# Seven half-size products instead of eight for 28 of the 40 column blocks of an input projection, with two intermediate results parked in DRAM and the spatial mixing moved under the output projection

## The chip, the core and the metric

The kernel runs on one core of one Trainium2 chip. The time is device microseconds (us) of one execution on that core. Before the change three runs took 1326.22, 1326.7 and 1324.02 us, median 1326.22 us. A profiled execution took 1324.03 us; its span from the first to the last instruction is 1322.2 us, with a mean granted TensorE clock of 0.992.

## What is computed

The reference runs two layers over 1,056 tokens (1,024 of a prompt and 32 of a running stream), each token a row of 1,024 float32 numbers. The change is in the first ("even") layer:

```
h = rms_norm(x, g_pre)
z = einsum('btd,de->bte', h, w_in)          # 1024 -> 5120 columns: 40 blocks of 128
a, uv, gate = z[..., :1024], z[..., 1024:3072], z[..., 3072:]
y_a = pool_mixer(a, ...)                    # trailing-window means, per-group linear, scale
u, v = split(gelu(uv));  v = layer_norm(v)
y_b = u * (W_s v + b)                       # spatial mixing over chunks of 128 positions
y = einsum('bte,ed->btd', concat(y_a, y_b) * silu(gate), w_out)     # 2048 -> 1024
x = x + rms_norm(y, g_post)
```

The odd layer (low-rank attention with its own input and output projections) follows and is not changed, apart from the buffers that it starts from.

## The kernel before

Everything lies transposed: channels on the 128 partitions, tokens along the free dimension. The 1,056 tokens are cut into a group "a" of 640 (two PSUM banks of 320) and a group "b" of 416 (one bank). Every product is made to float32 precision from two rounded parts of each operand: `hi` is the value rounded to the matmul's format, `lo` the rest, and hi·hi, hi·lo and lo·hi are summed in PSUM.

`prep_w` (L134) loads a weight block of 128 x 1024 in two pieces of 512 columns through the SP queue, ScalarE casts `hi` (L144), and GpSimd, or VectorE where it is told so, subtracts to get `lo` (L145). `mm_block` (L158) runs one block: 8 pieces of the contraction, 3 part products, 3 matmuls each (320, 320 and 416 columns), thus 72 matmuls, each with its own 128x128 weight load. `evac` (L182) has VectorE multiply the PSUM result by `rep`, the reciprocal root-mean-square of each token, spread over the partitions; `rstd` (L194) makes `rep`.

`even` (L286) goes through the blocks of w1 in this order: 8 and 9 while x arrives (L349-L357), block 10 (L367), the rest of u (11 to 15), v (16 to 23), the gates of half B (32 to 39), the pool inputs (0 to 7) and the gates of half A (24 to 31). v is transposed on TensorE (L424) into one buffer for each of nine token tiles; then `sgu` (L431) takes each tile: layer-norm statistics (L436-L440), normalising (L441), the hi/lo split (L445, L446), the spatial matmuls (L467, L468), a scale and bias by VectorE (L476, L477) and the multiplication of u by GpSimd (L479). This work is interleaved with the blocks of half B's gates and the pool inputs. u, v, the gates and the products stay in SBUF. Then the output projection runs over both halves (K = 16 pieces), first for group "a", then for "b" (L597-L616), and `residual` (L618) adds x, stores x1 to DRAM and makes the next layer's `hi`/`lo`; it runs under the next matmuls.

The order on TensorE is the program's, written by hand (`manual_schedule` on PE); the queues of the other engines are ordered by the framework from its own estimate of when each instruction can start. Side work comes in by tasks: `mm` adds its own price to a clock, `spawn` puts a task on a list with a due time, and `poll`, called after each contraction piece, advances the task that is due:

```
def mm(self, out, lhsT, rhs, start, stop, n):
    self.now += max(n / 2.4, 107)
```

The delays stand in the table `N` in ns of that clock: "lead" is the distance from one token tile of the spatial mixing to the next, "mix" the time from a tile's layer norm to its matmuls, "mixq" the distance between its four groups of matmuls, "tp", "tr", "res", "ra", "rb", "ha", "hb" are those of other tasks.

Of the kernel before, what the change touches and what calls it, by code (L numbers as in the profile page):

```python
# [19 lines left out]
P = 128  # L20
D = 1024
NK = 8
# [12 lines left out]
N = {"x": 462, "mix": 10626, "mixq": 1490, "tr": 717, "lead": 9945, "tr0": 11989, "res": 9194, "ra": 2699,  # L35
     "rb": 1574, "ha": 14000, "hb": 5000, "kv": 429, "q": 20908, "k": 34682, "kvs": 1773, "qs": 10662, "rest": 1357, "r1": 1608,
# [3 lines left out]
LU = 5  # L40
KS = 5
# [30 lines left out]
class Build:  # L72
    def __init__(self, ctx, tc, upto, aps):
        self.ctx, self.tc, self.nc = ctx, tc, tc.nc
        self.upto = upto
        for k, v in aps.items():
            setattr(self, k, v)
        self.uid = 0
        self.now = 0.0
        self.tasks = []  # L80
        self.rr = 0
        self.ca, self.nb = CA, NB
        self.banks = {}

# [35 lines left out]
    def bank(self, tag):  # L120

        tag, bufs = self.banks.get(tag, (tag, 2))
        return self.t(self.ps, [P, 2, 512] if tag in ("za", "sc") else [P, 512], F32, tag, bufs)
# [10 lines left out]
    def prep_w(self, src, n=1024, lo_on=None, pool=None):  # L134
# [3 lines left out]
        for o in range(0, n, 512):  # L138
            m = min(512, n - o)
            raw = self.t(self.stg, [P, 512], F32, "raw", bufs=3)  # L140
# [132 lines left out]
    def new_rep(self):  # L273
        return Pair(self.t(self.cst, [P, NA], F32, "repa"), self.t(self.cst, [P, NB], F32, "repb"))

    def sumsq(self, acc, src, first, g, eng, pool):
        nc = self.nc
        if first:
            nc.scalar.activation(acc, src, AF.Square)
        else:  # L280
            sq = self.t(pool, [P, NA if g == "a" else NB], F32, g)
            nc.scalar.activation(sq, src, AF.Square)
            eng.tensor_tensor(acc, acc, sq, ALU.add)


    def even(self):  # L286
        nc = self.nc
        self.ps = self.open("ps", bufs=2, space=PSUM)
        self.ab1 = self.open("ab1", bufs=24)
        evc = self.evc = self.open("evc")  # L290
        self.ab2 = self.open("ab2", side="right", bufs=9)
        self.V = self.open("V", side="right", bufs=9)


        xs = [self.t(self.V, [P, 1088], F32, "v") for _ in range(NK)]
# [18 lines left out]
        h = [None] * NK  # L314

        def split_x(g, k):
            x = xs[k][:, :NA] if g == "a" else xs[k][:, NA:T]
            if g == "a":
                h[k] = (self.pair(self.ab1, F32R, "a"), self.pair(self.ab1, F32R, "a"))
            else:  # L320
                for i in range(2):
                    h[k][i].b = self.t(self.ab1, [P, NB], F32R, "b")
# [11 lines left out]
        seq = list(range(8, 24)) + list(range(32, 40)) + list(range(8)) + list(range(24, 32))  # L334
        self.pos = 0

        def block(groups="ab", prep=True):
            b = seq[self.pos]
            self.pos += 1
            nb = seq[self.pos] if self.pos < len(seq) else None  # L340
            if prep and nb is not None and nb not in wts:
                wts[nb] = self.prep_w(self.i_w1[nb])
            return self.mm_block(self.wcol(wts[b]), h, range(NK), groups)


        mB = [None] * NK
        mB[0], mB[1] = (self.pair(self.ab2) for _ in range(2))

        for g in "ab":  # L349
            acc = self.t(self.ab2, [P, NA if g == "a" else NB], F32, g)  # L350
            z = [None, None]
            for k in range(NK):
                x = split_x(g, k)
                for i in range(2):
                    z[i] = self.mm_block(self.wcol(wts[8 + i]), h, [k], g, ps=z[i], first=k == 0, last=k == 7)
                self.sumsq(acc, x, k == 0, g, nc.vector, self.ab2)
# [3 lines left out]
        wts[10] = self.prep_w(self.i_w1[10], lo_on=nc.vector)  # L360
        self.pos = 2
        mB[2] = self.pair(self.ab2)
        for g, z in (("a", zz), ("b", z)):
            for i in range(2):
                self.evac(z[i], mB[i], rep, g)
                self.act(mB[i], AF.Gelu, g)
            ps = self.mm_block(self.wcol(wts[10]), h, range(NK), g)  # L367
            self.drain()
            self.evac(ps, mB[2], rep, g)
            self.act(mB[2], AF.Gelu, g)  # L370
        self.pos = 3
        wts[11] = self.prep_w(self.i_w1[11])
        for m in range(3, 8):
            ps = block()
            mB[m] = self.pair(self.ab2)
            self.evac(ps, mB[m], rep)
            self.act(mB[m], AF.Gelu)


        ws = [self.t(self.stg, [P, 512], F32, "raw", bufs=3) for _ in range(2)]  # L380
        nc.sync.dma_start(ws[0], self.i_wsT)
        nc.sync.dma_start(ws[1], self.i_bsb)
        wst = ws[0].rearrange("p (h i) -> p h i", h=4)
        nc.gpsimd.memset(wst[64:128, :, 0:64], 0.0)

        wsp = [self.t(self.ab1, [P, 2, 2, P], F32R, "a") for _ in range(2)]
# [4 lines left out]
        rs = self.t(self.ps, [P, 512], F32, "mi")  # L391
        for e, w in enumerate(wsp):
            for j in range(2):
                nc.tensor.matmul(rs[:, e * 256 : e * 256 + 256], self.ones, w[:, :, j, :], start=j == 0, stop=j == 1)
        Cc = self.pair(self.ab2)

        def cview(m):
            return Cc.a[:, m * P : (m + 1) * P] if m < 5 else Cc.b[:, (m - 5) * P : (m - 4) * P]

        for m in range(NK):  # L400
            hd = slice((m // 2) * P, (m // 2 + 1) * P)
            nc.vector.scalar_tensor_tensor(cview(m), rs[:, hd], self.vec(LNB, m), ws[1][:, hd], ALU.mult, ALU.add)
        rss = self.t(self.ps, [P, 512], F32, "mi")
        for q in range(4):
            for j in range(2):
                nc.tensor.matmul(rss[:, q * 32 : (q + 1) * 32], self.ones[:32, :], wsp[q // 2][:32, q % 2, j, :32],
                                 start=j == 0, stop=j == 1)
        Cs = self.t(evc, [P, NK, 32], F32, "Cs")
        for m in range(NK):
            q = m // 2  # L410
            nc.vector.scalar_tensor_tensor(Cs[:, m, :], rss[:, q * 32 : (q + 1) * 32], self.vec(LNB, m),
                                           ws[1][:, q * P : q * P + 32], ALU.mult, ALU.add)


        vt = {}
        vtok = {}

        def transposes(half, t):
            n = P if t < 8 else 32
            if half == 0:  # L420
                vtok[t] = self.t(self.V, [P, 1088], F32, "v")
            pt = self.t(self.ps, [P, 512], F32, "mi")
            for q in range(4):
                nc.tensor.transpose(pt[:n, q * P : (q + 1) * P], vt[half * 4 + q].tok(t), self.ident)  # L424
            dst = vtok[t][:n, half * 512 : half * 512 + 512]
            if t % 2:
                nc.scalar.copy(dst, pt[:n])
            else:
                nc.vector.tensor_copy(dst, pt[:n])

        def sgu(t):  # L431
            n = P if t < 8 else 32
            v = vtok[t][:n, :D]
# [8 lines left out]
            hi, lo = self.pair(self.ab1, F32R), self.pair(self.ab1, F32R)  # L442
            for g, s in (("a", slice(0, NA)), ("b", slice(NA, D))):
                w = s.stop - s.start
                nc.scalar.copy(hi.get(g)[:n, :w], v[:, s])  # L445
                nc.gpsimd.tensor_tensor(lo.get(g)[:n, :w], v[:, s], hi.get(g)[:n, :w], ALU.subtract)  # L446
            if t == 8:
                for g, s in (("a", slice(0, NA)), ("b", slice(NA, D))):
                    w = s.stop - s.start
                    lg, lb = (self.t(self.ab1, [P, NA if g == "a" else NB], F32, g) for _ in range(2))  # L450
                    nc.sync.dma_start(lg[:32, :w], self.i_lnbc[:, s])
                    nc.sync.dma_start(lb[:32, :w], self.i_lnbc[:, D + s.start : D + s.stop])
                    nc.vector.tensor_tensor(lg[:32, :w], lg[:32, :w], v[:, s], ALU.mult)
                    nc.vector.tensor_tensor(lg[:32, :w], lg[:32, :w], lb[:32, :w], ALU.add)
                    nc.scalar.dma_start(self.o_sv[:, s], lg[:32, :w])
            yield N["mix"]

            for q in range(4):
                mp = self.t(self.ps, [P, 2, 2, P], F32, "mi")
                w = wsp[q // 2][:n, q % 2, :, :n]  # L460
                for i in range(2):
                    m = q * 2 + i

                    def vs(pr):
                        return pr.a[:n, m * P : (m + 1) * P] if m < 5 else pr.b[:n, (m - 5) * P : (m - 4) * P]

                    self.mm(mp[:, i, :, :n], vs(hi), w, True, False, 2 * n)  # L467
                    self.mm(mp[:, i, 0, :n], vs(lo), w[:, 0, :], False, True, n)  # L468
# [4 lines left out]
                for i in range(2):  # L473
                    m = q * 2 + i
                    c = cview(m) if t < 8 else Cs[:, m, :]
# [3 lines left out]
                    nc.gpsimd.tensor_tensor(u, u, tmp[:, i], ALU.mult)  # L479

        def transpose_task(half):
            for t in range(9):
                transposes(half, t)
                yield N["tr"]
            if half:
# [746 lines left out]
```

## Time and profile before

| what | value |
|---|---|
| runs | 1326.22, 1326.7, 1324.02 us |
| the profiled execution | 1324.03 us, span 1322.2 us |
| VectorE, ScalarE and GpSimd busy | 53%, 38% and 29% of the span |
| read from and written to DRAM | 85.49 MB, 18.91 MB |
| w1's blocks after the first three (11 to 39, 0 to 7), with the pool and spatial work among them | 50.51 to 533.7 us |
| output projection | 533.7 to 725.8 us |
| first blocks of the odd layer, group a | 725.8 to 764.6 us |

In the profile PE is TensorE's matmul, PEld its weight load, DVE VectorE, ACT ScalarE, POOL GpSimd, SP the queue that issues loads. A matmul's listed duration holds its passage through the pipeline, and matmuls overlap, so the pace is read from one start to the next. The same holds to a lesser degree for VectorE: the next instruction starts some tens of ns before the end of the one ahead of it.

### The profile page before, as it was taken

How to read it: one execution, taken by the hardware profiler on the slowest of the kernel's cores; microseconds unless marked ns; L12 is line 12 of the kernel's file. 1: busy time of each engine (PE TensorE's matmuls, PEld its weight loads, DVE VectorE, ACT ScalarE, POOL GpSimd, SP SyncE). 2: the span in 40 equal slices, each digit the busy share in tenths (PEclk: the TensorE clock that was granted, in tenths of full speed). 3: DMA queues.
4: the chain of work that ended last, by engine and by line, in shares of the span. 5: the costliest groups of instructions: out<-in, count | busy, mean ns of one | idle time of the engine just before them, and what ended most of it. 6: DMA issues, size and time to landing. Idle time of an engine off the chain costs nothing.

```text
span 1322.2 us, 20987 instructions
## 1 busy us (share of the span) xinstructions
PE 1289.3 (98%) x8152; PEld 1257.9 (95%) x8152; DVE 703.0 (53%) x1370; ACT 496.3 (38%) x974; POOL 389.0 (29%) x443
## 2 busy tenths in 40 slices
PE   9999999999999999999999989999999999999995
PEld 8899999999999999999999989999999999999994
DVE  7311123967956344432286642743666666765438
ACT  7321222322132243322154322434656565655431
POOL 0321212678643222200001354322223323232410
PEclk9999999999999999999999989999999999999998
DMA  5111111111111111222256333322111111116525
GB/s 193 64 49 57 41 41 49 41 40 33 53 40 49 52 41 49 69 75 74 86 185 206 107 116 99 120 82 67 46 44 54 40 54 51 46 50 195 159 88 197
DMA packets 64226, 105.75 MB, mean 80 GB/s; under 512 B 9408, under 2 KB 27232, under 8 KB 64128
## 3 DMA queue, kind: packets, MB, share of 16 engines
q1 hardware_dynamic: 52496, 89.31, 21.9%
q10 hardware_dynamic: 11632, 15.11, 3.2%
q8 instruction: 64, 1.05, 0.3%
q14 instruction: 34, 0.28, 0.1%
HBM read 85.49 MB, written 18.91 MB: 79 GB/s over the span
## 4 chain that ended last, share of the span: by engine, by line
PE 85%; DVE 8%; issue 2%; DMA 1%; POOL 1%; ACT 1%; SPq 0%; ACTq 0%; DVEq 0%; POOLq 0%
PE za L109 36%; PE zb L109 20%; PE sc L109 12%; PE pj L109 11%; PE pj L906 2%; PE mi L109 1%; DMA raw<-in_wout 1%; PE mi L203 1%; PE mi L424 1%; DVE a L1129 1%; ACT sw L830 1%; DVE wlo L145 1%; DVE b L660 0%; DVE b L638 0%; DVE b L649 0%
## 5 line engine op out<-in xcount | busy, mean ns | idle before, releaser
L109 PE MATMUL za<-a,whi 128*128 128x320 f32 x2112 | 463.2, 313 | 2.5 <-DVE a L186 1.4
L109 PEld LDWEIGHTS za<-a,whi 128*128 128x128 f32 x2112 | 371.4, 189 | 5.9 <-DVE a L186 1.8
L144 ACT CAST whi<-raw 128x512 fp32r<-128x512 f32 (+2 forms) x240 | 145.5, 608 | 538.0 <-PE zb L109 255.0
L145 POOL TENSOR_TENSOR wlo<-raw,whi 128x512 fp32r<-128x512 f32 (+2 forms) x166 | 219.1, 1321 | 429.6 <-ACT whi L144 417.2
L109 PE MATMUL zb<-b,whi 128*128 128x416 f32 x1024 | 336.3, 352 | 2.0 <-DVE b L188 1.5
L109 PE MATMUL za<-a,wlo 128*128 128x320 f32 x1056 | 241.5, 310 | 0.0
L109 PEld LDWEIGHTS zb<-b,whi 128*128 128x128 f32 x1024 | 191.4, 188 | 3.3 <-DVE b L188 1.6
L109 PEld LDWEIGHTS za<-a,wlo 128*128 128x128 f32 x1056 | 191.9, 188 | 0.5
L109 PE MATMUL zb<-b,wlo 128*128 128x416 f32 x512 | 179.8, 351 | 1.6 <-DVE wlo L145 1.6
L186 DVE TENSOR_TENSOR a<-za,repa 128x640 f32<-128x640 f32 x38 | 31.1, 820 | 162.7 <-PE za L109 162.7
L879 POOL TENSOR_SCALAR p<-p,nm 128x128 f32<-128x128 f32 (+8 forms) x72 | 53.1, 738 | 163.2 <-DVE nm L878 128.5
L109 PEld LDWEIGHTS zb<-b,wlo 128*128 128x128 f32 x512 | 96.8, 189 | 2.3 <-DVE wlo L145 1.9
L145 DVE TENSOR_TENSOR wlo<-raw,whi 128x512 fp32r<-128x512 f32 x74 | 50.6, 688 | 68.4 <-ACT whi L144 68.2
L211 POOL TENSOR_TENSOR sm<-sm,mhalf 32x1 f32<-32x1 f32 (+3 forms) x17 | 15.6, 926 | 235.7 <-DVE sm L210 235.7
L877 ACT ACTIVATE p<-sc,nm 128x128 f32<-128x128 f32 (+8 forms) x72 | 50.6, 703 | 44.5 <-DVE nm L876 35.1
L109 PE MATMUL sc<-a,whi 128*128 128x400 f32 x256 | 57.6, 346 | 0.2 <-ACT p L877 0.2
L909 DVE TENSOR_TENSOR pl<-pj,ph 128x512 fp32r<-128x512 f32 (+2 forms) x96 | 51.1, 552 | 7.0 <-ACT ph L908 6.3
L876 DVE TENSOR_REDUCE nm<-sc 128x1 f32<-128x128 f32 (+8 forms) x72 | 50.7, 704 | 3.2
L908 ACT CAST ph<-pj 128x512 fp32r<-128x512 f32 (+2 forms) x96 | 43.8, 480 | 20.5 <-PE pj L906 18.1
L109 PEld LDWEIGHTS sc<-a,whi 128*128 128x128 f32 x256 | 46.4, 188 | 0.8 <-ACT p L877 0.4
L109 PE MATMUL pj<-pl,vh 128*128 128x256 f32 (+1 forms) x160 | 45.1, 282 | 0.2 <-DVE pl L909 0.2
L109 PE MATMUL pj<-ph,vl 128*128 128x256 f32 (+1 forms) x160 | 45.0, 281 | 0.0
(285 smaller groups left out, 2251.5 us busy)
## 6 DMA issues: line engine op xcount, KB each, us to landing
raw<-in_w SPq DMA_DIRECT2D x120, 256.0 KB, 2.7
raw<-in_wout SPq DMA_DIRECT2D x60, 256.0 KB, 3.1
gt<-gated SPq DMA_DIRECT2D x32, 128.0 KB, 2.4
ogd<-og ACTq DMA_DIRECT2D x32, 128.0 KB, 2.6
raw<-in_wo SPq DMA_DIRECT2D x16, 256.0 KB, 2.9
raw<-in_wok SPq DMA_DIRECT2D x16, 256.0 KB, 2.7
v<-in_xT SPq DMA_DIRECT2D x16, 208.0 KB, 4.4
rawa<-x1d SPq DMA_DIRECT2D x8, 400.0 KB, 3.7
```

What stands on the lines that cost most here:

```text
L109: self.nc.tensor.matmul(out, lhsT, rhs, start=start, stop=stop)
L144: nc.scalar.copy(hi[:, :m], raw[:, :m])
L145: (lo_on or nc.gpsimd).tensor_tensor(lo[:, :m], raw[:, :m], hi[:, :m], ALU.subtract)
L186: nc.vector.tensor_tensor(two(dst.a), ps[0][:, :, :CA], two(rep.a), ALU.mult)
L203: nc.tensor.matmul(st[:w, j : j + 1], acc[:, j * P : j * P + w], self.one, start=True, stop=True)
L211: nc.gpsimd.tensor_tensor(m[:w, c0:c1], m[:w, c0:c1], self.mhalf[:w, c0:c1], ALU.pow)
L876: nc.vector.tensor_reduce(nm[:n, 0:1], view, axis=AX.XY, op=ALU.max, negate=True)
L877: nc.scalar.activation(pv, view, AF.Exp, bias=nm[:n, 0:1], accum_out=nm[:n, 1:2])
L879: nc.gpsimd.tensor_scalar(p[:n, :K], p[:n, :K], nm[:n, 2:3], 1.0, ALU.mult, ALU.mult)
L906: nc.tensor.transpose(tr[:, e, :], p[:, (b + e) * P : (b + e + 1) * P], self.ident)
L908: nc.scalar.copy(hi[:, :nb, off : off + P], tr[:, :nb, :])
L909: nc.vector.tensor_tensor(lo[:, :nb, off : off + P], tr[:, :nb, :], hi[:, :nb, off : off + P], ALU.subtract)
```

## The change

**Seven products.** 28 blocks of w1 (u 10 to 15, v 16 to 23, the gates 24 to 31 and 34 to 39) are made in 14 pairs. A pair is a 2x2 block product: two output blocks by two halves of the contraction (4 pieces of 128 each), times two halves of the contraction by two halves of the tokens (`HT` = 528). Winograd's form takes seven products of half-size operands. A product (`product`) is 4 pieces x 3 part products x 2 matmuls of `HQ` = 264 columns: 24 matmuls, so 168 for a pair where two blocks had 144. The token-side sums (`th`, `tl`) are made once by `t_prep`; the weight-side sums and their `hi`/`lo` by `s_prep`, three products ahead, all `lo` on VectorE; results go through three PSUM tiles of two banks in turn and are summed by VectorE and ScalarE in `pair_block`, which multiplies by `rep` at the end. Blocks 8, 9, 32 and 33 stay ordinary and run first, blocks 0 to 7 stay ordinary and run last, in the order 6, 7, 4, 5, 2, 3, 0, 1.

**Through DRAM.** The products u·silu(gate) of half B go to `mBd`, the gates of half A to `gAd`, v (transposed as before) to `vd`. They are loaded again where they are used; v has one buffer, so a tile's load waits until the tile before it is split.

**Below the output projection.** The pool blocks now end in the multiplication by the loaded gate and the `hi`/`lo` split (`y_a`). The output projection starts with half A: m = 0 and 1 for group a, with the last pool group's `y_a` between, then m = 2 to 7, m = 2 to 5 (`BOTH`) for both groups. Below these run the loads of u and v and the spatial mixing. When five tiles are done, half B follows for group a and is added to the saved half; the other four tiles, then `split_b`, come below that; last comes group b, with half A's share for m = 6, 7, 0, 1. `residual` and `odd_in` are the same work in other buffers.

The SBUF is laid out in numbered slots (`L`, `R`) instead of rotating pools. The diff, cut to its core:

```
+N = {"tp": 5500, "sa": 9000, "sl": 12000, "sb": 6000, "sbk": 2000, "sg": 500, "x": 462, "mix": 10626, "mixq": 1490, "tr": 717, "lead": 9500, "tr0": 11989, "res": 9194, "ra": 2699,
+     "rb": 1574, "ha": 8000, "hb": 5000, "kv": 429, "q": 20908, "k": 34682, "kvs": 1773, "qs": 10662, "rest": 1357, "r1": 1608,
...
+HT, HQ = 528, 264
+RAW = 3
+LO_POOL = ()
+BOTH = (2, 3, 4, 5)
+A_ORDER = [6, 7, 4, 5, 2, 3, 0, 1]
...
+        def t_prep():
+            for k in range(4):
+                q = [[xs[k + 4 * i][:, j * HT : (j + 1) * HT] for j in range(2)] for i in range(2)]
+                for i in range(2):
+                    nc.scalar.activation(xs[k + 4 * i][:, :T], xs[k + 4 * i][:, :T], AF.Copy, scale=self.vec(GA1, k + 4 * i))
+                tt = nc.vector.tensor_tensor
+                tt(q[0][0], q[0][1], q[0][0], ALU.subtract)
...
+                for n, (j, e, o, f) in place.items():
+                    hi, lo = X[n](k)
+                    src = xs[k + o][:, f * HT : (f + 1) * HT]
+                    nc.scalar.copy(hi, src)
+                    tt(lo, src, hi, ALU.subtract)
+                yield N["tp"]
...
+        pairs = [(10, 11), (34, 35), (36, 37), (12, 13), (14, 15), (38, 39)] + [(24 + 2 * i, 25 + 2 * i) for i in range(4)]
+        pairs += [(16 + 2 * i, 17 + 2 * i) for i in range(4)]
...
+        def s_prep(q):
...
+            if n == 1:
+                for e in ("s1", "s2"):
+                    w[e] = self.t(self.stg, [P, 512], F32, "raw", bufs=RAW)
+                tt(w["s1"], w["21"], w["22"], ALU.add)
+                tt(w["s2"], w["s1"], w["11"], ALU.subtract)
+            elif n == 4:
+                tt(w["21"], w["11"], w["21"], ALU.subtract)
+            elif n == 5:
+                tt(w["s2"], w["12"], w["s2"], ALU.subtract)
...
+            nc.scalar.copy(hi, src)
+            lo_on.tensor_tensor(lo, src, hi, ALU.subtract)
...
+        def product(q, x):
+            out = zt[q % 3]
+            wh, wl = wq.pop(q)
+            s_prep(q + 3)
...
+            for k in range(4):
+                xh, xl = x(k)
+                c = slice(k * P, (k + 1) * P)
+                for j, (w, xx) in enumerate(((wh, xh), (wh, xl), (wl, xh))):
+                    for e in range(2):
+                        self.mm(out[:, e, :HQ], w[:, c], xx[:, e * HQ : (e + 1) * HQ], k == j == 0,
+                                k == 3 and j == 2, HQ)
+                self.poll()
+            return out[:, :, :HQ]
+
+        def pair_block(p, d1, d2):
+
+            a1, b1, a2, b2 = (two(v) for d in (d1, d2) for v in (d[:, :HT], d[:, HT:T]))
+            tt = nc.vector.tensor_tensor
+            q = 7 * p
+            nc.scalar.copy(a1, product(q, X["11"]))
+            tt(b1, product(q + 1, X["t2"]), a1, ALU.add)
+            tt(a1, product(q + 2, X["21"]), a1, ALU.add)
+            nc.scalar.copy(b2, product(q + 3, X["t1"]))
+            tt(a2, product(q + 4, X["t3"]), b1, ALU.add)
+            tt(b1, b1, b2, ALU.add)
+            tt(b2, b2, a2, ALU.add)
+            tt(b1, product(q + 5, X["22"]), b1, ALU.add)
+            tt(d1[:, :T], d1[:, :T], rep.w, ALU.mult)
+            tt(a2, product(q + 6, X["t4"]), a2, ALU.add)
+            tt(d2[:, :T], d2[:, :T], rep.w, ALU.mult)
...
+            if p >= vstart:
+                self.spawn(v_task(p - vstart, d), N["tr0"])
+            elif 24 <= b0 < 32:
+                for e in range(2):
+                    nc.scalar.dma_start(gAd[b0 - 24 + e], d[e][:, :T])
...
+        def load_v(t):
+            n = P if t < 8 else 32
+            vt[t] = R(0)[:, :D]
+            nc.sync.dma_start(vt[t][:n], vd[t, :n])
+
+        load_v(0)
...
+        for k in range(NK):
+            nc.sync.dma_start(mB[k].w, mBd[k])
...
+            nc.vector.tensor_tensor(lo, v, hi, ALU.subtract)
+            if t + 1 < 9:
+                load_v(t + 1)
             yield N["mix"]
...
+        for m in range(2, NK):
+            w = wn.pop(m)
+            if m < 7:
+                wn[m + 1] = self.prep_w(self.i_wout[m + 1, :, :1024])
             else:
...
+            ps = self.mm_block(self.wcol(w), mix, A_ORDER, "ab" if m in BOTH else "a")
+            put(m, ps)
+        while len(done) < 5:
+            self.step(min(self.tasks, key=lambda t: t[:2]))
+        split_a()
```

More of the change, by code (lines that the diff above doesn't have):

```diff
@@ L273, in new_rep, with sumsq @@
     def new_rep(self):
-        return Pair(self.t(self.cst, [P, NA], F32, "repa"), self.t(self.cst, [P, NB], F32, "repb"))
-    def sumsq(self, acc, src, first, g, eng, pool):
+        return self.halves(self.t(self.cst, [P, T], F32, "rep"))
+    def sumsq(self, acc, src, first, g, eng, sq):
         nc = self.nc
@@ L313, in even @@
         rep = self.new_rep()
-        h = [None] * NK
+        h = [tuple(halves(L(2 * k + e, F32R)) for e in range(2)) for k in range(NK)]
         def split_x(g, k):
             x = xs[k][:, :NA] if g == "a" else xs[k][:, NA:T]
[L318 to L322, printed above, removed]
             hi, lo = h[k][0].get(g), h[k][1].get(g)
@@ L332, in even @@
         state = self.t(evc, [P, NK, 30], F32, "state")
[L334 to L343, printed above, removed]
@@ L363, in even @@
+        for i in range(4):
+            s_load(0, i)
         for g, z in (("a", zz), ("b", z)):
             for i in range(2):
[L365 to L377, printed above, removed]
@@ L380, in even @@
[L380 to L383, printed above, removed]
+                self.evac(z[i], u01[i], rep, g)
+                nc.scalar.activation(u01[i].get(g), u01[i].get(g), AF.Gelu)
+            if g == "a":
+                tp = self.spawn(t_prep(), N["tp"])
+            for i in range(2):
+                ps = (zt[i], None) if g == "a" else (None, zt[2][:, i, :])
+                if g == "b" and i == 1:
+                    s_prep(0)
+                    s_prep(1)
+                self.mm_block(self.wcol(wts[32 + i]), h, range(NK), g, ps=ps)
+                if i == 0 and g == "a":
+                    while any(t[2] is not tp[2] for t in self.tasks):
+                        self.step(next(t for t in self.tasks if t[2] is not tp[2]))
+                self.evac(ps, g01[i], rep, g)
@@ new lines, in even, with pslot @@
+        self.h2 = [(Pair(None, None), Pair(None, None)) for _ in range(NK)]
+        zs = [zt[(7 * len(pairs) + i) % 3] for i in range(3)]
+        self.zrot = [[zs[0], zs[2]], [zs[1][:, i, :] for i in range(2)]]
+        self.shut(self.lb)
+        lb = self.lb = self.open("lx")
+        mix = {}
+        pfree, held = list(range(9)), {}
+        def pslot(who, dt=F32):
+            i = pfree.pop(0)
+            held.setdefault(who, []).append(i)
+            return R(i, dt)
+        gslot = dict(zip(A_ORDER, (16, 17, 4, 5, 6, 7, 8, None)))
@@ new lines, in even, with put @@
+        nc.scalar.dma_start(self.o_st, state)
+        yp = self.yp = [halves(L(m)) for m in range(NK)]
+        def put(m, ps):
+            nc.scalar.copy(two(yp[m].a), ps[0][:, :, :CA])
+            if m in BOTH:
+                nc.scalar.copy(yp[m].b, ps[1][:, :NB])
+        part = {}
+        for m in range(2):
+            if m == 1:
+                wA1 = self.prep_w(self.i_wout[1, :, :1024])
+            part[m] = self.mm_block(self.wcol(wA if m == 0 else wA1), mix, A_ORDER[:6], "a", last=False)
@@ new lines, in even @@
+        B2 = zs[1]
+        y_a(pg, wp[pg], lambda: (B2, self.t(self.ps, [P, 512], F32, "mi")))
+        for m in range(2):
+            self.mm_block(self.wcol(wA if m == 0 else wA1), mix, A_ORDER[6:], "a", ps=part[m], first=False)
+            put(m, part[m])
+        wn = {2: self.prep_w(self.i_wout[2, :, :1024])}
+        mB = [halves(L(8 + k)) for k in range(NK)]
+        vt = {}
+        def load_v(t):
+            n = P if t < 8 else 32
+            vt[t] = R(0)[:, :D]
+            nc.sync.dma_start(vt[t][:n], vd[t, :n])
@@ L400, in even @@
[L400 to L407, printed above, removed]
-        Cs = self.t(evc, [P, NK, 32], F32, "Cs")
@@ L409, in even @@
[L409 to L422, printed above, removed]
-            for q in range(4):
[L424 to L429, printed above, removed]
+        Cc = R(8)
@@ L479, in sgu, with sgu_task @@
                     nc.gpsimd.tensor_tensor(u, u, tmp[:, i], ALU.mult)
-        def transpose_task(half):
+            done.append(t)
+        done = []
+        def sgu_task():
+            yield from spatial()
             for t in range(9):
-                transposes(half, t)
-                yield N["tr"]
-            if half:
-                for t in range(9):
-                    yield from sgu_lead(t)
-        def sgu_lead(t):
-            self.spawn(sgu(t), 0)
-            yield N["lead"]
@@ L618, in residual, with split_a @@
-    def residual(self, g, acc, y, h2):
+                self.spawn(sgu(t), 0)
+                yield N["lead"]
+            self.spawn(split_b(), N["sb"])
+        k0 = [halves(R(6 + i, F32R)) for i in range(2)]
+        def split_a():
+            for k in range(NK):
+                hi, lo = (v.a for v in (mix[A_ORDER[k - 1]] if k else k0))
+                mix[8 + k] = (Pair(hi, None), Pair(lo, None))
+                nc.scalar.copy(hi, mB[k].a)
+                nc.vector.tensor_tensor(lo, mB[k].a, hi, ALU.subtract)
```

499 lines of the change are left out of this document (322 added, 177 removed).

## The prediction

> **What bounds the kernel.** I read the page's span, busy shares and chain first, then what TensorE waited for, then a table of stages.
>
> ```profile
> span 1322.2 us, 20987 instructions
> PE 1289.3 (98%) x8152; PEld 1257.9 (95%) x8152; DVE 703.0 (53%) x1370; ACT 496.3 (38%) x974; POOL 389.0 (29%) x443
> PE 85%; DVE 8%; issue 2%; DMA 1%; POOL 1%; ACT 1%; SPq 0%; ACTq 0%; DVEq 0%; POOLq 0%
> ```
> ```profile
> PE mi L203 <- DVE b L660: 5.8, 1, 5.8
> ```
> ```profile
> 34.00:50.50 16.50, 13.53 (x86) 13.15 (x86) 7.74 (x18) 5.86 (x9) 6.27 (x9) 1.00 0.20 65
> 62.16:73.81 11.65, 11.65 (x75) 11.61 (x74) 1.32 (x2) 2.42 (x5) 2.59 (x2) 1.00 0.14 46
> 168.70:313.20 144.50, 144.50 (x942) 143.02 (x941) 86.53 (x166) 38.46 (x66) 69.16 (x82) 1.00 0.13 41
> 646.40:700.00 53.60, 51.55 (x276) 50.08 (x276) 41.67 (x69) 23.92 (x38) 1.57 (x3) 1.00 0.55 175
> ```
>
> TensorE is the bound: busy 98% of the span, 85% of the chain, and its longest wait for another engine is 5.8 us. In the stage table the columns are the stretch, its length, then PE, PEld, DVE, ACT and POOL busy, the granted clock, the DMA share and GB/s. The stretch 62.16 to 73.81 is one clean block of w1: 11.65 us, PE full, DVE idle for nine tenths. So in this stage only fewer or shorter matmuls save time, and DVE has room to pay for it. In the output projection (646.40) DVE is busy 41.67 of 53.60 us and DMA runs at 175 GB/s: there is less room there.
>
> **The products.** Does a matmul of 264 columns cost 264/320 of one of 320?
>
> ```profile
> 154.31 0.46 PE L109 MATMUL za<-a,whi 128*128 128x320 f32 x2
> 154.61 0.34 PE L109 MATMUL zb<-b,whi 128*128 128x416 f32 x1
> 154.79 0.46 PE L109 MATMUL za<-a,whi 128*128 128x320 f32 x2
> ```
> ```profile
> 1192.19 0.28 PE L109 MATMUL pj<-ph,vh 128*128 128x256 f32 x1
> ...
> 1192.91 0.28 PE L109 MATMUL pj<-ph,vh 128*128 128x256 f32 x1
> ```
> ```profile
> 1189.51 0.29 PE L109 MATMUL pj<-qh,wlo 128*128 128x288 f32 x1
> 1189.64 0.29 PE L109 MATMUL pj<-qh,whi 128*128 128x288 f32 x1
> ```
>
> Two of 320 take 0.30 us, one of 416 takes 0.18. Between the first and the last row of 256 columns lie six starts, so 0.72 / 6 = 0.120 us each; 288 columns take 0.13. In between, 264 columns take 0.120 + 8/32 x 0.010 = 0.1225 us. A pair was 2 x 11.65 = 23.30 us; it becomes 168 x 0.1225 = 20.58, a gain of 2.72, and 14 pairs gain 38.1 us. The bounds are the neighbouring rows: at 0.120 a pair is 20.16 (43.9 us gained), at 0.130 it is 21.84 (20.4 us). I take the middle value, since 256 is much the nearer width.
>
> The Trainium skill, "TensorE: Matmul & The Clock Gate", section "Back-to-back issue gap", gives N/2.4 + 2.5 ns; by it a pair would go from 21.5 to 18.9 us, an estimate of 36 us for all. The trace's own pace is some 8% slower than that page's, at every width.
>
> All other TensorE work is the same in number: as many transposes, pool products, spatial matmuls and output columns as before. The stretch 168.70 to 313.20 held 11 blocks (128.2 us by the clean one), so 16.3 us of transposes and spatial work; they move to the v pairs and below the output projection and cost the same there. Taken as 0, with -6 to +6 for waits between them.
>
> **Does VectorE keep up with the pairs?**
>
> ```profile
> 33.48 1.28 DVE L145 TENSOR_TENSOR wlo<-raw,whi 128x512 fp32r<-128x512 f32 x2
> 34.68 1.54 DVE L186 TENSOR_TENSOR a<-za,repa 128x640 f32<-128x640 f32 x2
> ```
> ```profile
> L145 DVE TENSOR_TENSOR wlo<-raw,whi 128x512 fp32r<-128x512 f32 x74 | 50.6, 688 | 68.4 <-ACT whi L144 68.2
> L186 DVE TENSOR_TENSOR a<-za,repa 128x640 f32<-128x640 f32 x38 | 31.1, 820 | 162.7 <-PE za L109 162.7
> L144 ACT CAST whi<-raw 128x512 fp32r<-128x512 f32 x220 | 136.1, 620 | 521.2 <-PE zb L109 243.9 <-PE za L109 97.6 <-issue 87.6
> L192 ACT ACTIVATE a<-a 128x640 f32<-128x640 f32 x32 | 23.6, 739 | 22.6 <-DVE a L186 22.6
> ```
> ```profile
> 34.04 1.28 ACT L192 ACT_TABLE_LOAD   x1
> ```
>
> Two in a row take 1.28 us where one lasts 0.688, so the pace is 0.59 us at 512 columns; in the same way 0.72 at 640, a slope of 1.02 ns per column. That makes 0.61 at 528, 1.15 at 1,056 and 0.49 at 416. A pair asks DVE for 4 sums and 7 `lo` of 512 (6.5 us), 5 sums with PSUM and 2 in SBUF of 528 (4.3) and 2 multiplications by `rep` (2.3): 13.1 us of 20.58. Three pairs add two gate products (2.3), the four v pairs 3 copies (1.8). The last three products of a pair carry most: 3 `lo`, 2 weight sums, 5 token sums, 2 multiplications, 8.3 us (10.6 with gates) against 3 x 2.94 = 8.8 us of PE. PSUM holds three products, so a result may be late by two, 5.9 us, and the next window is light. ACT has 7 casts of 0.62, two copies and two activations of about 1.1, some 8 us, plus a table load of 1.28 us whenever gelu follows silu. All covered on average; the handoffs at a pair's end I price at 0.2 us, 3 us for 14 pairs. Bounds: 0 if all hides, 14 at a microsecond each.
>
> **The entry.** Product 1 needs the token sums of all four pieces. `t_prep` gives DVE 32 instructions of 528 (19.5 us). Until it ends DVE also has the work that the row 34.00 to 50.50 shows (7.7), `lo` of blocks 32 and 33 (4 x 0.59 = 2.4), three more evacuations (1.7), the first three `s_prep` (5 x 0.59 = 3.0) and two gate products (2.3): 36.6 us from 34.0, to 70.6. PE needs two blocks from 35.5 (23.3 us, and 1.7 of `rstd` matmuls) to 60.5, product 0 to 63.4, and the last piece of product 1 at 65.6. A wait of 5 us, 6 with handoffs; 0 if DVE's order is kinder, 15 if ACT's casts hold it up.
>
> After a wait that long the clock may drop:
>
> ```profile
> 764.60:779.50 14.90, 9.10 (x48) 8.80 (x47) 8.54 (x18) 3.85 (x7) 6.13 (x9) 0.77 0.51 155
> ```
>
> Behind the 5.8 us wait the granted clock averages 0.77 over this stretch, but most of the slow time was the wait itself. The Trainium skill, same page, section "Part 1: The HAM clock gate", says that an idle window of about 3.4 us halves the clock until a busy one has passed; by that this entry would cost up to 2 us more. The row agrees, and the upper end takes it in.
>
> **The spatial mixing.** One buffer for v makes each tile a chain: load, statistics, GpSimd's power, normalise, cast, subtract, and only then the next load.
>
> ```profile
> cos<-in_cos SPq DMA_DIRECT2D x1, 528.0 KB, 4.2
> gb<-in_gp2bc SPq DMA_DIRECT2D x1, 512.0 KB, 5.0
> sin<-in_sin SPq DMA_DIRECT2D x1, 528.0 KB, 3.4
> ```
> ```profile
> L436 DVE BATCH_NORM_STATS2 bs<-v 128x6 f32<-128x512 f32 x16 | 10.6, 669 | 1.1 <-ACT v L427 1.1
> L441 DVE TENSOR_SCALAR v<-v,sm 128x1024 f32<-128x1024 f32 x8 | 7.4, 930 | 0.4
> L440 POOL TENSOR_TENSOR sm<-sm,mhalf 128x1 f32<-128x1 f32 x8 | 4.3, 543 | 13.7 <-DVE sm L439 13.7
> ```
>
> Load 4.2 us, two statistics 1.3, aggregate and add 0.3, power 0.5, normalise 0.9, cast of 1,024 1.1 (by the two ACT rows' slope), subtract 1.1: 9.4, with handoffs about 10.3 us. The plan sets tiles 9,500 ns apart on its own clock; a clean block is 24 x 1,056 / 2.4 = 10.56 us on it and 11.65 on the chip, so a tile has 10.5 us. Chain and plan are about equal. The eight loads of u (4.3 MB, 25 us at 175 GB/s) go out around the same time, and tile 1 and the weights of m = 3 queue behind them on SP. I price this at 7 us, nearer to the low end since chain and plan come out equal: 0 if the u loads start early under the last pool product, 27 if each tile takes 14 us (9 x 14 less 99 us of cover: 9 x 10.5 and about 4.5 of lead). Waiting in SP's queue behind a v load are weight loads (PE then waits for them); behind TensorE's wait on a tile stand the output matmuls.
>
> **Joins.** Between half A's first matmuls and the last pool group, and at `split_a`, the `hi`/`lo` of the next piece follow late results: 2 us, from 0 to 6. The group b part brings fewer matmuls over the same `residual` work; its 5.8 us wait stays. Taken as 0.
>
> **The sum**, against the profiled execution's own 1324.0 us: -38.1 + 3 + 6 + 7 + 2 = -20.1, so 1303.9. The runs' median is 2.2 us above that execution, so the forecast for a median is 1306.
>
> **The rivals.**
>
> *All covers hold.* The waits come to 6 us instead of 18: 1324.0 - 38.1 + 6 + 2.2 = 1294. For it speaks that PE was kept 98% busy with DVE at 86.53 of 144.50 us in the mixing stage; against it the entry, where DVE's work adds up to more than PE's.
>
> *The tile chain sets the pace of the output projection* (slower). If a tile takes 16 us (a 5.0 us load, queued behind weights; DVE busy with other tiles' scale and bias), PE waits 9 x 16 - 99 = 45 us: 1324.0 - 38.1 + 11 + 45 + 2.2 = 1344. It decides from 9c - 99 = 27, c = 14 us. For it: load and chain are serial, and the row 646.40 shows DMA and DVE already loaded. Against: the rows add up to 10.3.
>
> *VectorE sets the pace of the pairs* (slower). If a pair takes 23 us, the gain there is 4 and the rest costs 15: 1324.0 - 4 + 15 + 2.2 = 1337. From 22.2 us on nothing is left. For it: the last three products' 8.3 to 10.6 us. Against: two products of slack in PSUM.
>
> *Weight loads set the pace*, so that the change does not do what it says: 168 loads where 144 stood, 27.2 us per pair, 54 us slower, 1399. The 256-column rows, each with a load of its own, start 0.120 us apart and speak against it. The Trainium skill, same page, section "LDWEIGHTS", puts a load of 128 columns at 107 ns, still under that pace.
>
> **The numbers.** A difference of 0.2% (2.7 us) is about what a measurement can tell. Forecast (1299 to 1320) 0.45; all covers hold (1284 to 1299) 0.3; gain eaten up (1320 to 1330) 0.1, of which 0.06 lies within 0.2%; tile chain 0.08, VectorE 0.05, weight loads 0.02. Faster 0.45 + 0.3 + 0.03 = 0.78, same 0.06, slower 0.16. The range leaves out the dearest ends of the slower cases and the cheapest of the fast one: 1288 to 1330.
>
> **What would show it.** Right: 14 stretches of 20 to 21 us for 168 matmuls of 264 columns, starts 0.12 us apart; one wait of some 5 us at product 1 for `lo` of the token sums; small waits below the output projection on v's `hi`/`lo`. Wrong: starts at 0.13 or more; gaps at each pair's end for a PSUM tile that VectorE holds; TensorE waiting at every tile of the mixing; a chain that runs through v's loads.

## The result and the profile after

The changed kernel takes 1367.3 us (median of 4 runs, 1365.11 to 1368.61) where the kernel before takes 1326.46 beside it: a ratio of 1.031, 95% interval 1.029 to 1.0329. It is slower by 40.8 us; the prediction had said 1306 us. The profiled execution took 1365.11 us.

The head of the page after, with span, busy shares and the chain:

```profile
span 1363.2 us, 22025 instructions
...
PE 1269.6 (93%) x8488; PEld 1228.1 (90%) x8488; DVE 860.6 (63%) x1613; ACT 552.2 (41%) x1027; POOL 306.0 (22%) x381
...
PE 25%; DVE 3%; issue 1%; ACT 1%; DMA 1%; POOL 0%; DVEq 0%; ACTq 0%; POOLq 0%
```

TensorE fell from 98% to 93% busy, and its share of the chain from 85% to 25%. The percentages of the chain after no longer add up to the span: the chain is followed back from one release to the next and here it breaks off, so it says little, and the waits have to be read instead. What TensorE waited for, after (total, times, longest):

```profile
PE z L116 <- DVE l L199: 15.3, 9, 5.6
PE z L116 <- DVE r L589: 7.1, 7, 1.2
PE z L116 <- DVE l L856: 5.9, 4, 3.1
PE mi L214 <- DVE r L907: 5.3, 1, 5.3
PE z L116 <- DVE l L854: 5.3, 3, 3.7
PE z L116 <- DVE b L623: 4.9, 4, 1.6
```

Before, the only long wait was one of 5.8 us. Now TensorE waits for VectorE in ordinary blocks: L199 and L589 are evacuations, in the odd layer's gates and in the pool blocks. The stage table after (stretch, length, PE, PEld, DVE, ACT and POOL busy, clock, DMA share, GB/s) shows where that happens and where it doesn't:

```profile
35.87:46.45 10.58, 10.55 (x62) 10.32 (x62) 9.16 (x22) 8.20 (x12) 7.30 (x6) 0.84 0.01 3
64.70:289.60 224.90, 224.90 (x1849) 224.90 (x1849) 163.58 (x234) 86.78 (x127) 0.00 (x0) 1.00 0.26 91
356.90:486.60 129.70, 115.60 (x705) 111.43 (x704) 75.92 (x105) 30.14 (x57) 38.63 (x45) 1.00 0.25 79
663.10:741.90 78.80, 64.09 (x315) 60.46 (x315) 49.27 (x84) 29.98 (x48) 8.22 (x10) 0.93 0.50 159
826.40:948.00 121.60, 106.58 (x638) 103.42 (x636) 48.10 (x99) 34.07 (x61) 28.85 (x36) 0.96 0.24 78
```

The second row holds the first eleven pairs: PE is full for 224.90 of 224.90 us, 20.44 us per pair. The third is the pool blocks, which the change was not meant to touch: eight blocks and three `y_a` products. A clean block is 11.65 us and a `y_a` product (half a block) 5.8, so 110.6 us would do (8 x 11.65 + 3 x 5.8); it took 129.7, and VectorE was busy for only 75.92 of them. The fourth row is group b's part of the output projection, and the first belongs to the entry; both are taken up below. The last row is the odd layer's gates, with VectorE busy 40% and TensorE with 15 us of idle time. The timeline of one pool block's start shows what is wrong (start, length, engine, line, operation; in brackets the idle time before it and who ended it):

```profile
368.64 0.46 PE L116 MATMUL z<-l,whi 128*128 128x320 f32 x2
368.65 0.82 DVE L587 TENSOR_TENSOR r<-z,rep 128x640 f32<-128x640 f32 x1 [9.43 <-PE z L116]
369.39 0.55 DVE L588 TENSOR_TENSOR r<-z,rep 128x384 f32<-128x384 f32 x1
369.86 0.18 DVE L589 TENSOR_TENSOR r<-z,rep 128x32 f32<-128x32 f32 x1
370.10 0.94 PE L116 MATMUL z<-l,whi 128*128 128x416 f32 x4 [0.99 <-DVE r L589]
```

Block 7's first two matmuls, for group a, start at 368.64. The third is its first matmul for group b, and it waits until VectorE has read out block 6's group b (384 and 32 columns). Block 7 writes another accumulator than the one that is read: group b has two, in turn. But the changed kernel makes these two out of one PSUM tile. The lines are in the diff, outside the core shown above:

```
+        zs = [zt[(7 * len(pairs) + i) % 3] for i in range(3)]
+        self.zrot = [[zs[0], zs[2]], [zs[1][:, i, :] for i in range(2)]]
```

Of the three two-bank tiles that the products went through, two become group a's accumulators, and the two halves of the third become group b's. Before, `zb` was two tiles of one bank. My theory (A): a matmul into one half is made to wait for the reader of the other half, because they are one tile to the framework that sets the waits, and each block then loses what VectorE needs to read out its predecessor. The rivals (B): the loss is the spatial mixing below the output projection, or VectorE's added work, whoever shares a tile.

### The profile page after: what moved, and what is told of

The parts are those of the page before. It is cut to its first block, busy times and chain, and to the rows that moved or that the text cites. A ratio compares the mean times of both kernels' runs of the same rounds, so it can differ in the third digit from the quotient of the medians.

```text
span 1363.2 us, 22025 instructions
## 1 busy us (share of the span) xinstructions
PE 1269.6 (93%) x8488; PEld 1228.1 (90%) x8488; DVE 860.6 (63%) x1613; ACT 552.2 (41%) x1027; POOL 306.0 (22%) x381
## 5 line engine op out<-in xcount | busy, mean ns | idle before, releaser
L116 PE MATMUL z<-l,whi 128*128 128x264 f32 (+2 forms) x2032 | 395.2, 308 | 31.8 <-DVE l L199 15.3
L116 PEld LDWEIGHTS z<-l,whi 128*128 128x128 f32 x2032 | 319.1, 191 | 39.5 <-DVE l L199 16.6
L116 PE MATMUL z<-l,wlo 128*128 128x264 f32 (+2 forms) x1240 | 269.0, 301 | 0.0
L155 ACT CAST whi<-raw 128x512 fp32r<-128x512 f32 (+1 forms) x180 | 108.1, 603 | 352.5 <-PE z L116 221.1
L116 PEld LDWEIGHTS z<-l,wlo 128*128 128x128 f32 x1240 | 203.5, 191 | 0.3
L116 PE MATMUL z<-r,whi 128*128 128x264 f32 (+2 forms) x696 | 152.8, 307 | 15.6 <-DVE l L854 5.3
L116 PE MATMUL z<-a,whi 128*128 128x320 f32 x704 | 145.2, 312 | 1.5 <-ACT a L625 0.7
L116 PEld LDWEIGHTS z<-r,whi 128*128 128x128 f32 x696 | 114.5, 191 | 19.2 <-issue 4.8
L116 PEld LDWEIGHTS z<-a,whi 128*128 128x128 f32 x704 | 116.1, 188 | 2.9 <-ACT a L625 0.9
L116 PE MATMUL z<-a,wlo 128*128 128x320 f32 x352 | 80.2, 309 | 0.0
```

What stands on the lines that cost most here:

```text
L116: self.nc.tensor.matmul(out, lhsT, rhs, start=start, stop=stop)
L155: nc.scalar.copy(hi[:, :m], raw[:, :m])
```

## The experiments

**Own tiles for group b.** After the products, the pool of PSUM tiles is closed and another opened in its place, with four tiles:

```
-        zs = [zt[(7 * len(pairs) + i) % 3] for i in range(3)]
-        self.zrot = [[zs[0], zs[2]], [zs[1][:, i, :] for i in range(2)]]
+        self.shut(self.zp)
+        self.zp = self.open("zq", space=PSUM)
+        yb = [self.t(self.zp, [P, 512], F32, f"y{i}", 1) for i in range(2)]
+        ya = [self.t(self.zp, [P, 2, 512], F32, f"y{i + 2}", 1) for i in range(2)]
+        self.zrot = [[ya[1], ya[0]], yb]
```

An instruction that had used both halves at once (the last `y_a`'s evacuation, the squares of half B) becomes two. What was expected:

> The seven products are as in the changed kernel; after them, group b's two accumulators are two PSUM tiles of their own instead of the two halves of one tile. Theory A (shared tile: the next block's first group-b matmul waits until the block before it is evacuated, although it writes the other half): the waits of 1.2 us per pool block go, those of the gates and of the output projection's group b mostly too, together some 45 us by the wait table: about 1322 us. Theory B (VectorE is late in these stages, whatever the buffers): the waits stay or move to the next buffer, under 12 us gained: 1355 us or more.

Measured: 1313.02 us (1311.62 to 1314.14), ratio to before 0.9901, interval 0.9884 to 0.9918; 54.3 us less than the changed kernel, and more than the 45 that theory A took from the listed waits (a wait as listed is less than what it costs, see below). The same block start in this run, then its stage table (pool blocks, group b's part of the output projection, gates), then what TensorE waited for:

```profile
371.60 1.13 PE L125 MATMUL y<-l,whi 128*128 128x320 f32 x6
371.61 0.82 DVE L600 TENSOR_TENSOR r<-y,rep 128x640 f32<-128x640 f32 x1 [9.43 <-PE y L125]
...
372.36 0.55 DVE L601 TENSOR_TENSOR r<-y,rep 128x384 f32<-128x384 f32 x1
...
372.58 0.64 PE L125 MATMUL y<-l,wlo 128*128 128x320 f32 x3
```
```profile
359.87:472.00 112.13, 112.13 (x705) 111.36 (x704) 77.52 (x104) 30.36 (x57) 39.53 (x45) 1.00 0.28 92
644.78:711.66 66.88, 59.13 (x314) 56.40 (x314) 51.34 (x85) 29.27 (x48) 8.61 (x10) 0.97 0.58 189
795.16:900.00 104.84, 104.84 (x669) 104.08 (x668) 49.65 (x101) 37.34 (x68) 31.10 (x37) 1.00 0.28 96
```
```profile
PE y L125 <- DVE b L877: 5.6, 1, 5.6
PE mi L223 <- DVE r L924: 5.3, 1, 5.3
PE mi L125 <- DVE tm L780: 4.3, 2, 2.9
PE mi L125 <- DVE dgh L780: 2.5, 2, 1.3
PE mi L125 <- DVE dgl L780: 2.2, 2, 1.6
PE z L125 <- DVE r L206: 2.1, 1, 2.1
PE z L125 <- DVE r L208: 2.0, 1, 2.0
```

Block 7's matmuls run on from 371.60 without a gap (a third of them, with 416 columns, for group b), while VectorE reads block 6: its group a from 371.61, its group b from 372.36 (L601). The pool blocks take 112.13 us with PE full: 17.6 of the 54 us come back here. The gates are full as well, and group b's part of the output projection (the row 644.78) is 12 us shorter. Of the waits at the evacuation of a block, the two at the entry (L206, L208) are left, and some 2 us in group b's output (L871, L873, not shown). The new tiles take the place of the pool that was closed, the matmuls are the same, VectorE is busy for 866.1 us where it was for 860.6, and the mean granted clock is 0.985 where it was 0.984: what goes is the wait. How the framework comes to set it was not looked into; the runs show that sharing a tile decides.

**The other side: one shared tile in the kernel before.** The first trial gave group b's two accumulators of the kernel before as halves of one tile. In it group b of pool blocks 2, 4 and 6 and of the first gate of half A was overwritten by a `y_a` product ahead of its evacuation, by the order of the code, which makes the output wrong; the work is otherwise whole.

```
+        if tag == "zb" and not self.banks:
+            self.zh.append(self.zh.pop(0))
+            return self.zh[-1]
...
+        zh = self.t(self.ps, [P, 2, 512], F32, "zb", 1)
+        self.zh = [zh[:, i, :] for i in range(2)]
```

The edit also replaces tiles that are taken anew for each block by halves that live throughout. The accumulators of the changed kernel live throughout in both of its forms, shared and own, so that alone does not make them wait.

> The kernel before, with one thing changed: group b's two accumulators are the two halves of one PSUM tile. Theory A (shared tile): each block that uses them waits for the evacuation of the block before it. Some 37 blocks of w1, 8 pool products, 8 outputs and 8 gates of the odd layer, 1.2 us each where VectorE is free at once and up to 5 us where it is not: 60 to 110 us slower, 1385 to 1435 us. Theory B (VectorE late whatever the buffers, or something in the new layout): 1326 us, no change.

Measured: 1411.15 us, ratio 1.0634 (1.0595 to 1.0674). A second trial has the same edit behind a change of order (a pool block's evacuation told ahead of the `y_a` product), so that nothing is overwritten, and that order alone is its control.

> The kernel before, with only the order of statements changed, so that in a block that GpSimd evacuates the evacuation is told ahead of y_a's product. The control for the run beside it. Both theories: no difference, 1326 us within 8.

> The control with one edit: group b's two accumulators become the two halves of one PSUM tile in place of two tiles; the computation is whole. Theory A (the shared tile makes each block's first product into one half wait for the evacuation of the other half): slower by 55 to 90 us than the control, 1381 to 1416 us, with waits of about 1 us of TensorE on VectorE at the first group-b product of each block. Theory B (the loss of the changed kernel came from elsewhere, such as the spatial mixing below the output projection or the token sums): 1326 us within 8.

Measured: the control 1326.61 us (ratio 1.0002, 0.9987 to 1.0017), with the shared tile 1411.58 us (ratio 1.0645, 1.0614 to 1.0677). One declaration costs 85 us in a kernel that has none of the rest of the change. TensorE's longest wait in the control, and the main ones with the shared tile:

```profile
PE mi L203 <- DVE b L664: 5.8, 1, 5.8
```
```profile
PE zb L109 <- DVE b L191: 36.2, 31, 5.6
PE zb L109 <- DVE v L525: 8.8, 8, 2.6
PE zb L109 <- DVE v L191: 6.5, 7, 0.9
PE zb L109 <- ACT b L556: 6.4, 7, 1.2
```

In the second fence 53 waits of about 1.1 us stand at `zb`, group b's accumulator: one at nearly every block. They are 57.9 us together. Two more rows of that list stand at `zb`, 4.7 us in six waits (L623) and one of 4.4 (L285), while the control has 3.3 us there in all: 63.7 us more than the control. The wait as listed is less than what a block loses: after, pool block 3 with a wait of 0.99 us took 12.86 us from its first start to the next block's (452.48 to 465.34), and 11.62 with own tiles (443.18 to 454.80), 1.24 more. By that factor 63.7 us of waits are 80 us of time, an estimate, of the 85 measured.

**Without the products.** The kernel with own tiles, but the 14 pairs as 28 ordinary blocks and no token sums.

```
-        def t_prep():
...
+            for e, d in enumerate((d1, d2)):
+                nb = flat[2 * p + e + 1]
+                wts[nb] = self.prep_w(self.i_w1[nb], lo_on=nc.vector)
+                ps = self.mm_block(self.wcol(wts.pop(flat[2 * p + e])), h, range(NK))
+                self.evac(ps, halves(d), rep)
```

> As e1_own_banks, but the 14 pairs are computed as 28 ordinary blocks and the token sums are left out: the new order, the storage in DRAM and the mixing below the output projection without the products. The seven products alone are worth 14 x (23.3 - 20.44) = 40 us less what the entry costs (about 4): 36 us slower than e1. Theory A: about 1358 us. Theory B: about 1395 us.

Measured: 1354.39 us, ratio 1.0215 (1.0194 to 1.0235). The products bring 1354.4 - 1313.0 = 41.4 us. Some 1.7 of it lies at the entry, which ends at 69.4 us here and at 67.7 with the products: in this kernel blocks 32 and 33 have tiles of their own too, and TensorE waits 6.2 us for the spread of `rep` (L241) instead. Everything else that the change does (parking in DRAM, the mixing's new place, the new order) costs 28.6 us over the 1325.75 of the kernel before, even with own tiles.

**Without the spatial mixing.** The kernel with own tiles; v's statistics, its products and the multiplication of u are left out, so u goes on unmixed.

```
-            load_v(0)
...
-                    self.mm(mp[:, i, :, :n], hi[:, c], w, True, False, 2 * n)
-                    self.mm(mp[:, i, 0, :n], lo[:, c], w[:, 0, :], False, True, n)
```

> As e1_own_banks, without the spatial mixing (no loads of v, no layer norm of v, no spatial matmuls, and u times gate goes on unmixed). TensorE loses 14 us of matmuls. If the mixing costs only these, 14 us faster than e1. If VectorE's lateness in the mixing holds TensorE up (theory B: waits of 5 to 12 us in either half of the output projection), 30 us or more faster than e1.

Measured: 1287.04 us, so the mixing costs 26 us where it is, between the two cases that were expected. In the kernel with own tiles a group of four mixing matmuls delays the next block's matmuls by this much:

```profile
540.15 0.35 PE L125 MATMUL y<-b,wlo 128*128 128x416 f32 x1
540.34 0.57 PE L125 MATMUL mi<-r,r 128*128 128x256 f32 x4
540.75 0.50 PE L125 MATMUL y<-a,whi 128*128 128x320 f32 x2
541.09 0.35 PE L125 MATMUL y<-b,whi 128*128 128x416 f32 x1
```

0.41 us to the next start, and 0.04 more to the one after it (0.34 us between the last two rows, where two matmuls of 320 take 0.30): 0.45 us for each of 32 groups, 14.4 us. The four groups of the short ninth tile and the twelve matmuls that set the mixing up take some 4.5 us more, read in the same way. In the list of waits above, 9.0 us stand at `mi` with L780 as their end: the mixing's PSUM bank, which VectorE has still to read. That makes some 28 where 26 were measured; the kernel without the mixing has small waits that the other has not, such as 1.4 us for `whi` (L164). So most of the 26 are matmuls, and about a third is waiting.

**The entry and the scratch.** In the kernel with own tiles, two more places shared a PSUM tile: blocks 32 and 33 for group b were two halves of one product tile, and the squares of the last residual used, as scratch, the tile that the odd layer's first block needs.

```
-                ps = (zt[i], None) if g == "a" else (None, zt[2][:, i, :])
+                ps = (zt[i], None) if g == "a" else (None, zt[2 * i][:, 0, :])
...
-        za = self.zrot[0][0]
+        za = self.zrot[0][1]
```

> e1_own_banks with the two waits of the same kind that are left: blocks 32 and 33 of group b go to two PSUM tiles instead of two halves of one (waits of 2 us at the entry), and the squares of group b's outputs go to the accumulator that the odd layer takes second instead of first (a wait of 5.6 us). Theory A: 7 to 8 us faster than e1, about 1305 us. Theory B: VectorE is late there and the wait moves to the next buffer: under 2 us.

Measured: 1310.43 us (1309.83 to 1311.72), ratio 0.9877 (0.9852 to 0.9901): 2.6 us instead of 7 to 8, and little more than the runs can tell, since the interval overlaps that of the kernel with own tiles. What this kernel waited for in the first pair (64 to 90 us):

```profile
PE z L125 <- DVE r L404: 1.3, 1, 1.3
PE z L125 <- ACT l L403: 0.4, 1, 0.4
```

The 2.0 us at L208 and the 5.6 us at L877 are gone. In their place comes this wait for the token sums at product 1, which takes the first pair from 20.51 to 22.74 us, and in the odd layer's first blocks one of 2.1 us for the spread of its `rstd`. Most of what was freed seems to have been given back at the next thing that was late.

**Less on VectorE.** The last kernel with the `lo` of half B's and group b's output weights on GpSimd.

```
-                wn = self.prep_w(self.i_wout[m + 1, :, 1024:], lo_on=nc.vector)
+                wn = self.prep_w(self.i_wout[m + 1, :, 1024:])
...
```

> e4_entry_scratch with the lo parts of half B's and group b's output weights subtracted by GpSimd instead of VectorE. If VectorE's load sets the pace of the output projection (theory B for this stage: its busy share is 60.7 of 73.7 us in half B's group a), VectorE loses 11 to 12 us there and the stage gets 5 us or more faster. If it is the handing over between engines, no gain, or a loss since GpSimd takes 1.3 to 1.4 us for what VectorE does in 0.6: 0 to 8 us slower.

Measured: 1315.03 us (1311.48 to 1316.03), 4.6 above the kernel that it was made from; the ratios to before, 0.9903 (0.9870 to 0.9935) and 0.9877, overlap in their intervals, so what is shown is that nothing was gained. Its waits from 490 to 705 us:

```profile
PE mi L125 <- DVE dgh L780: 4.6, 2, 3.5
PE mi L125 <- DVE tm L780: 4.1, 2, 3.3
PE y L125 <- POOL wlo L165: 2.3, 2, 1.5
...
PE mi L125 <- DVE dgl L780: 1.4, 2, 0.8
```

VectorE is busy for 145.57 us from 492 to 705 where it was for 158.65, and the waits on the mixing's bank stay at about 10 us; those for GpSimd's `wlo` are new. That speaks against VectorE's work in sum setting the pace of that part. It does not settle it, since GpSimd's lateness came in its place.

**The mixing later.** The plan's clock counts 10.56 us for a block that takes 11.65 on the chip, so it might bring TensorE to the mixing products too early. The delays times 1.103:

```
-N = {... "mix": 10626, "mixq": 1490, ... "lead": 9500, ...
+N = {... "mix": 11720, "mixq": 1640, ... "lead": 10480, ...
```

> The kernel with own tiles for group b and the squares' scratch moved, with the mixing plan's delays raised by 10.3% (11720 for 10625, 1640 for 1490, 10480 for 9500). Theory A (the plan's clock runs some 10% ahead of the chip, 10.56 us against 11.65 us a block, so TensorE comes to the mixing products before VectorE has freed the mixing's PSUM bank): the waits on the mixing's bank, 4.3 and 2.5 us in the output projection, go, and the kernel gains 3 to 5 us on 1310.4, to 1306. Theory B (VectorE has too much to do in that stage, wherever the products are put): 1310 within 2, the waits move to other products.

Measured: 1310.46 us (1309.51 to 1312.56), no difference. From 480 to 660 us the waits on the mixing's bank:

```profile
PE mi L125 <- DVE dgl L780: 5.3, 3, 2.2
PE mi L125 <- DVE dgh L780: 2.4, 2, 1.4
PE mi L125 <- DVE tm L780: 0.8, 1, 0.8
```

Without the edit the three were 4.3, 2.4 and 2.2 us, for `tm`, `dgh` and `dgl`: 8.9 us became 8.5, on other products. The plan's clock is not the cause. Neither of these two runs found what is; that VectorE comes to these short reads late because longer work (statistics, normalising, residual) stands ahead of them in its queue fits the rows but was not tried.

## Why the prediction was wrong

**The step that failed** is "All other TensorE work is the same in number [...] Taken as 0, with -6 to +6 for waits between them", and with it "The group b part [...] Taken as 0". The number was right (8,488 matmuls in the profile after and with own tiles alike, the 8,152 of before and 14 x 24 for the products); the waits were not. The change also altered which PSUM tile the untouched blocks accumulate in, a part that the prediction did not list and so did not price. It costs 54.3 us, shown from both sides: taken out of the changed kernel, and put into the kernel before, where it costs 85. None of the rivals held it. The likeliest of the slower ones, at 1344 us, was a chain through v's loads; none of TensorE's listed waits after is for a load. The nearest that the prediction came was its sign "gaps at each pair's end for a PSUM tile that VectorE holds": such gaps came, but in the blocks that were not to change.

The Trainium skill, "PSUM — Partial Sum Buffer", section "PSUM bank collisions raise a hardware error", asks for a guard between engines by bank and quadrant, and says that accesses to different banks run clean. The two halves here were different banks, and the run with own tiles in the same place agrees: VectorE reads group b's one bank from 372.36 us while TensorE goes on into the other without a gap. So the wait was not one that the memory asked for.

**The products: right.** From 119.76 to 120.86 us the profile after has nine starts of 264 columns:

```profile
119.76 0.28 PE L116 MATMUL z<-l,whi 128*128 128x264 f32 x1
119.88 0.40 PE L116 MATMUL z<-r,whi 128*128 128x264 f32 x2
120.12 0.41 PE L116 MATMUL z<-l,wlo 128*128 128x264 f32 x2
120.37 0.65 PE L116 MATMUL z<-l,whi 128*128 128x264 f32 x4
120.86 0.41 PE L116 MATMUL z<-l,wlo 128*128 128x264 f32 x2
```

1.10 / 9 = 0.122 us, where 0.1225 was said. A pair takes 20.44 us (20.58 said), so 14 pairs gain 14 x (23.30 - 20.44) = 40.0 us (38.1 said), and the run without products gives 41.4. The rivals of weight loads and of VectorE's pace fall: the profile after lists no wait of TensorE between 64 and 357 us, and VectorE is 73% busy over the first eleven pairs. The 3 us of handoffs were 0.

**The entry: size near, cause another.** 6 us were said for a wait at product 1. With own tiles the first pair starts at 67.72 us, after four blocks; before, three blocks ended at 50.51, and a fourth would end at 62.16. That is 5.6 us, but they came from the shared tile of blocks 32 and 33 (the 2.0 us at L208) and from a slower clock (below). The forecast wait showed as 1.7 us only when that sharing was taken away, so the size was near by luck.

**The mixing: 9 us of waits where 7 were said, of another kind.** So the size is luck. They are at the mixing's PSUM bank, and no wait is for a load or for v's `hi` and `lo`.

**Joins and group b.** 2 us were said for joins and 0 for group b. At the first join 1.2 us of waits are listed with own tiles (L637, L640, L641). Group b's twelve half blocks would take 54.7 us at 4.56 each (24 matmuls of 416 columns at 0.19 us); with own tiles they take 66.88, 12 us more, of which 5.6 were the scratch. The kernel before also lost there: 79.40 us, from 646.40 to 725.80, for eight blocks of 9.12, 6.4 more. So against before it is 6 us, about what the scratch took. With the scratch moved the part takes 62.00 us (643.40 to 705.40), 7 more than clean, so the 0 nearly held where no tile was shared.

**The sum by measured terms**: -41 for the products, +54 for the shared tile, and +28.6 for the rest. These are differences between runs, one after the other, so that they come to the measured +41 by construction; what tests the working is the rest, 28.6 us where 18 were said. Of it the rows name, against the kernel before, 8 for the mixing (9.0 less the 1.2 that before had at `mi`), 6 for group b and 6 for the entry: 20. Some 9 are not named. The clock has a share in them: its mean was 0.992 before and 0.985 with own tiles, which is up to 0.007 x 1312 = 9 us, an estimate, part of it in the entry's 6. Without the shared tile the kernel takes 1313 us, 7 above the forecast and inside its range: there the products brought 3 us more than was said and the rest cost 11 more, so that the range held with some luck.

The fastest version here is the one with the tiles separated in all three places: 1310.4 us, 1.2% under the kernel before (interval 1.0 to 1.5%).

## What to carry to other kernels

When a change moves accumulators, look at how the tiles are declared, not only at where they lie: two buffers in turn made from halves of one tile are one buffer to whatever sets the waits, and each block then pays the read-out of the one before (1.24 us on a block of 11.6 here, 54 us in all). "The same work in other buffers" is a claim about waits, and it needs its own line in the sum. And an engine that is idle for 41% of a stage, as VectorE was in the pool blocks after (busy 75.92 of 129.70 us), can still hold up another, if the free time isn't where the hand-over is.

## What the runs showed of the hardware that was not expected

The clock halved after a short wait. In the kernel with the tiles separated in all three places, TensorE waited 2.12 us ahead of block 32:

```profile
36.20 0.83 PE L125 MATMUL z<-l,whi 128*128 128x320 f32 x4 [2.12 <-DVE r L206]
...
38.64 1.43 PE L125 MATMUL z<-l,whi 128*128 128x320 f32 x4
...
42.01 1.27 PE L125 MATMUL z<-l,whi 128*128 128x320 f32 x4
```

```profile
36.17:48.06 11.89, 11.86 (x62) 11.76 (x62) 9.15 (x22) 8.48 (x12) 7.55 (x6) 0.71 0.01 4
```

From 38.64 to 42.01 us lie 12 starts, 0.28 us each, where a matmul of 320 columns takes 0.15 elsewhere. The stretch was granted a clock of 0.71; its 62 matmuls took 11.89 us here and 10.58 after (clock 0.84 in the stage table above), with the same wait of 2.1 us ahead of them. The records of the granted clock in the two traces hold one stretch at 0.50 there, 6.83 us long here and 3.41 us after. Half of that is lost, some 3.4 us here and 1.7 after, an estimate, besides the wait itself; why it is the longer one here and the shorter one there, behind waits that are alike, was not tried. In all eleven traces each stretch at half clock, but for the one at the program's end, has one of these two lengths. With that end, they come to 22.3 us before, 47.1 after and 42.7 with the tiles separated. The Trainium skill, "TensorE: Matmul & The Clock Gate", section "Part 1: The HAM clock gate", puts the idle window that halves the clock at about 3.4 us; here 2.1 us without a matmul were enough.
